# Three groups of projection tiles walk their weight rows in another order and at other places

## The chip, the cores and the metric

The kernel runs on one core of one Trainium2 chip. The metric is the device time of one execution in microseconds (us). The program's inputs and outputs lie in the chip's main memory (HBM); weights come in by DMA while the matrix engine (TensorE, "PE" in the profile) works on those that came before.

## The reference

One inference step of a hybrid decoder layer over 336 token columns: 16 meta tokens, 256 prompt tokens and 8 x 8 sample tokens. Cut to what matters here:

```python
h = rms_norm(x, norm_w)
proj = h @ w_in        # z | x,B,C | dt | B | C | h | SiLU gate | gate a | gate b
xbc = silu(causal_dwconv(xbc, conv_prev, ssd_conv_w) + ssd_conv_b)
y = ssd_chunked(xs, dt, log_a, bm, cm, state, chunk) + d_skip * xs
y_a = gated_group_rms_norm(y, z, ssd_norm_w) @ w_ssd_out
y_b = (sc_b * causal_dwconv(sc_c * sc_h) * silu(sc_z)) @ w_sconv_out
merged = sigmoid(g_a) * y_a + sigmoid(g_b) * y_b
out = rms_norm(x + merged @ w_o, final_norm_w)
```

The model width is 2048, so every projection sums over 16 blocks of 128 rows. All of it is float32.

## The kernel before

**Precision and tiles.** Each operand is split into a high and a low part that TensorE multiplies at its quicker float32 setting ("fp32r"): high by high, high by low, low by high. One output tile of 128 columns (`unit`, L136) takes the weights in two halves of 8 row blocks. For each half, `wblk` (L97) fetches 512 KB into `wraw` by a DMA on the SP queue, ScalarE (ACT) copies it to `whi`, and VectorE (DVE) writes the remainder to `wlo`. Then `mm` (L131) issues 24 matmuls: 3 passes over 8 row blocks. So one tile is 48 matmuls of 128x128 weights by 320, 324 or 336 token columns, all into one PSUM tile `pj`.

**Places in memory.** The row blocks of `whi` and `wlo` are `WS` = 144 floats (576 bytes) apart, and `spaced` (L94) puts the whole tile at a shift of 16 floats (64 bytes) times `at`. The token blocks of `hx` are 336 floats (1344 bytes) apart; tiles of 336 columns begin at a block's start, those of 324 columns 48 bytes further, and the projections of 320 columns 64 bytes further. The constants `AT_V`, `AT_Y`, `AT_O`, `AT_X`, `AT_U` = 1, 3, 3, 1, 2 (L91) are shifts.

**The walk.** `terms` (L117) lists the 24 matmuls of a half. A whole number as `plan` walks the eight row blocks upwards by one, starting at that number. A tuple walks by its step: `SEVEN` (L115) starts at block 6, goes down by two, and turns (a step of 7 or 5) so that odd and even blocks take turns in fours.

**Stages.** In order: an opening stage (L238) while the input arrives; 48 short-convolution tiles; the "gates" of branch b (L453 to L461), 16 gate tiles of 320 columns, each followed by a tile of `w_sconv_out` (`wsc`); the SSD stage, which weaves `z_units`, `conv_units`, `out_units` and the scan's own small matmuls over eight groups; then branch a's gates; and the last stage (L859 to L868), 14 tiles of `w_o` over the merged activations, with a short tail for the last 256 columns. In the SSD stage `conv_tile` (L477) projects the 32 "x tiles" (j below 32, four for each group) with 336 columns, the B tiles (j from 32) with 336, and the C tiles with 324.

**What orders the work.** Each engine runs its own list in order and waits on semaphores. The list is made by a scheduler in the tile layer that places instructions by its own estimates of when their inputs are ready. At the last stage's start L830 (ACT) and L831 (DVE) write the merged activations into `hx`, block 0 to block 15, and the matmuls of the first `w_o` tile read them.

Of the kernel before, what the change touches and what calls it, by code (L numbers as in the profile page):

```python
# [16 lines left out]
META = 16  # L17
TC = 12
TV = T - META
# [30 lines left out]
def tile_hybrid_step(ctx, tc, xT, w0, w1, w2, wdt, wso, wsc, wo, cmask, vec, hvec, convst, sconvst, xe_, fwe, h0T,  # L50
# [23 lines left out]
    hhi, hlo = hx[:, 0], hx[:, 1]  # L74
# [12 lines left out]
    def col(base, i):  # L87
        return V[:, base + i:base + i + 1]

    latest = {}  # L90
    AT_V, AT_Y, AT_O, AT_X, AT_U = 1, 3, 3, 1, 2  # L91
# [4 lines left out]
    def wblk(src, at=0):  # L96
        raw = wp.tile([P, 1024], F32, name="wraw")  # L97
        nc.sync.dma_start(raw, src)
        raw = raw.rearrange("p (k m) -> p k m", m=P)
        hi, lo = (spaced(name, at) for name in ("whi", "wlo"))  # L100
        latest["act"] = nc.scalar.activation(hi, raw, AF.Copy).ins  # L101
        latest["dve"] = nc.vector.tensor_tensor(lo, raw, fb(hi), sub).ins  # L102
        return hi, lo
# [11 lines left out]
    SEVEN, FIVE, ON = (6, (7, 5, 5, 5), -2), (6, (5, 5, 5, 5), -2), (None, (5, 5, 5, 5), -2)  # L115

    def terms(plan, half, hi, lo, xh, xl, nk):  # L117
        if not isinstance(plan, tuple):
            return [(w, x, (k + plan) % nk) for w, x in ((hi, xh), (hi, xl), (lo, xh)) for k in range(nk)]
        first, turns, step = plan  # L120
        k, out = first if half == 0 and first is not None else row[0] + step, []
        for i, (w, x) in enumerate(((hi, xh), (hi, xl), (hi, xl), (hi, xh), (lo, xh), (lo, xh))):
            if i in (2, 5):
                k += turns[2 * half + i // 5] - step
            for _ in range(4):
                out.append((w, x, k % nk))
                k += step
        row[0] = out[-1][2]
        return out

    def mm(out, hi, lo, xh, xl, base, nk, k0, first, last, plan=0, half=0):  # L131
        for i, (w, x, k) in enumerate(terms(plan, half, hi, lo, xh, xl, nk)):
            latest["pe"] = nc.tensor.matmul(out, w[:, base + k], x(k0 + k), start=first and i == 0,  # L133
                                            stop=last and i == 3 * nk - 1).ins

    def unit(src, xh, xl, n, plan=0, at=0):  # L136
        pt = ps.tile([P, 512], F32, name="pj")
        for half in range(2):
            hi, lo = wblk(src[:, half * 1024:half * 1024 + 1024], at)
            mm(pt[:, :n], hi, lo, xh, xl, 0, 8, half * 8, half == 0, half == 1, plan, half)  # L140
        return pt[:, :n]

    def proj(src, t0, plan=0, at=0):
        return unit(src, lambda k: hhi[:, k, t0:T], lambda k: hlo[:, k, t0:T], T - t0, plan, at)
# [44 lines left out]
    with tc.tile_pool(name="pa", bufs=2) as pa:  # L189
# [33 lines left out]
        for k in range(KT):  # L223
            split = nc.scalar.activation(uhi[:, k, :], ya[:, k, :], AF.Copy, scale=yan[:, k:k + 1])
            rest = nc.vector.scalar_tensor_tensor(ulo[:, k, :], ya[:, k, :], yan[:, k:k + 1], fb(uhi[:, k, :]), mult, sub)
            if k % 2 == 0:
                hi = wp.tile([P, WB], F32R, name="whi")
                lo = wp.tile([P, WB], F32R, name="wlo")
# [222 lines left out]

        tab = tables(pa)
        for m in range(KT):  # L453
            pg = proj(w2[80 + m], META)
            th = pa.tile([P, TV], F32, name="thg", tag="thz")
            nc.scalar.activation(th, pg, AF.Tanh, scale=0.5)
            py = unit(wsc[m], lambda k: vhi[:, k, :], lambda k: vlo[:, k, :], TV, 7, AT_V)
            nc.vector.scalar_tensor_tensor(th, th, 1.0, py, add, mult)
            nc.sync.dma_start(mb_d[m], th)
            next(tab, None)  # L460
# [6 lines left out]
    with tc.tile_pool(name="pb", bufs=2) as pb:  # L467
# [9 lines left out]
        def conv_tile(src, j, t0, out, cs):  # L477
            if t0:
                pp = proj(src, t0, SEVEN)
            else:  # L480
                pp = proj(src, t0, FIVE if j < 32 and j % 4 == 3 else SEVEN, AT_X)
            pad = pads[npad[0] % 2]
            npad[0] += 1
            smp = pad[:, 275:363].rearrange("p (b t) -> p b t", t=11)
            nc.scalar.activation(pad[:, 3 + t0:275], pp[:, :272 - t0], AF.Copy)  # L485
            nc.scalar.activation(smp[:, :, 3:11], pp[:, 272 - t0:].rearrange("p (b t) -> p b t", t=8), AF.Copy)
            nc.gpsimd.tensor_copy(smp[:, :, 0:3], cs[:, 1:9, :])  # L487
            nc.gpsimd.tensor_copy(cs[:, 0, :], pad[:, 272:275])  # L488
            nc.gpsimd.tensor_copy(cs[:, 1:9, :], smp[:, :, 8:11])
            i0 = META if t0 else 0  # L490
            acc = pb.tile([P, 360], F32, name="cacc")
            nc.scalar.activation(acc[:, i0:], pad[:, i0:360], AF.Identity, bias=col(V_CB, j), scale=col(V_CW, 4 * j))
            for k in range(1, 4):
                nc.vector.scalar_tensor_tensor(acc[:, i0:], pad[:, i0 + k:360 + k], col(V_CW, 4 * j + k),  # L494
                                               acc[:, i0:], mult, add)
            th = pb.tile([P, 360], F32, name="cth", bufs=1)
            nc.scalar.activation(th[:, i0:], acc[:, i0:], AF.Tanh)  # L497
            nc.vector.scalar_tensor_tensor(out[:, i0:272], th[:, i0:272], 1.0, acc[:, i0:272], add, mult)
            nc.vector.scalar_tensor_tensor(
                out[:, 272:].rearrange("p (b t) -> p b t", t=8),  # L500
                th[:, 272:360].rearrange("p (b t) -> p b t", t=11)[:, :, 3:11], 1.0,
                acc[:, 272:360].rearrange("p (b t) -> p b t", t=11)[:, :, 3:11], add, mult)

        def conv_units(g, st):
            cs = pb.tile([P, 6, 9, 3], F32, name="cs")
            nc.sync.dma_start(cs, convst[:, g])
            BT = st["BT"] = pb.tile([P, T], F32, name="BT")
            conv_tile(w1[64 + g], 32 + g, 0, BT, cs[:, 4])
            yield
            CT = st["CT"] = pb.tile([P, T], F32, name="CT")  # L510
            conv_tile(w1[72 + g], 40 + g, 12, CT, cs[:, 5])
            yield
            xs = st["xs"] = pb.tile([P, 4, T], F32, name="xs", tag=f"xs{g % 2}", bufs=1)
            for t in range(4):
                conv_tile(w1[32 + 4 * g + t], 4 * g + t, 0, xs[:, t, :], cs[:, t])
                yield
            nc.sync.dma_start(convo[:, g], cs)
# [19 lines left out]
        def ssd(g, st):  # L537
# [67 lines left out]
            def state(c, terms):  # L605
                pst = ps.tile([P, 512], F32, name="ms") if c == 2 else ps.tile([P, 4, 512], F32, name="yb", bufs=1)[:, 0]
                for i, (lhs, rhs) in enumerate(terms):
                    nc.tensor.matmul(pst, lhs, rhs, start=i == 0, stop=i == len(terms) - 1)  # L608
                if c:
                    nc.vector.tensor_tensor(hst[c], hst[c], pst, add)  # L610
                else:
                    nc.scalar.activation(hst[c], pst, AF.Copy)
# [215 lines left out]
    with tc.tile_pool(name="pc", bufs=3) as pc_:  # L828
# [30 lines left out]
        for m in range(KE):  # L859
            xr = pc_.tile([P, TV], F32, name="xr")  # L860
            nc.sync.dma_start(xr, xk[:, m, META:])
            po = unit(wo[m], lambda k: hhi[:, k, :TV], lambda k: hlo[:, k, :TV], TV, at=AT_O)
            nc.vector.scalar_tensor_tensor(ya[:, m, :TV], po, 0.5, xr, mult, add)
            s_ = pc_.tile([P, TV], F32, name="sqf") if m else sacc
            nc.scalar.activation(s_, ya[:, m, :TV], AF.Square)
            if m:
                nc.gpsimd.tensor_tensor(sacc, sacc, s_, add)  # L867
            nc.scalar.activation(ya[:, m, :TV], ya[:, m, :TV], AF.Copy, scale=col(V_FW, m))  # L868
        nc.sync.dma_start(xe[:, :PT], xe_)
        nc.sync.dma_start(fw[:, :PT], fwe.partition_broadcast(P))  # L870
        for m in range(KE, KT):
            xr = pc_.tile([P, TV], F32, name="xr")[:, :NA]
            nc.sync.dma_start(xr, xk[:, m, META:META + NA])
            po = ps.tile([P, 512], F32, name="pj")
            for half in range(2):
# [6 lines left out]
                for wide in ((True, False), (False, True))[half]:  # L882
                    for k in range(8):
                        w, x = (h, hx[:, :, 8 * half + k, :NA]) if wide else (l, hhi[:, 8 * half + k, :NA])
# [141 lines left out]
def _build(shapes):  # L1026
    import concourse.bacc as _bacc
    import concourse.tile as _tile

    nc = _bacc.Bacc("TRN2", target_bir_lowering=False, num_devices=1, dynamic_dma_scratch_size=8192)  # L1030
    args = [nc.dram_tensor(n, s, F32, kind="ExternalInput").ap() for n, s in shapes]
    args += [nc.dram_tensor(n, s, F32, kind="ExternalOutput").ap() for n, s in _OUTS]
    with _tile.TileContext(nc) as tc:
        tile_hybrid_step(tc, *args)
    return nc
# [23 lines left out]
```

## Time and profile before

| | |
|---|---|
| median of 2 runs | 1780.62 us (1780.04 to 1781.2) |
| the profiled execution | 1779.76 us |
| its span, first to last instruction | 1777.9 us |
| PE busy / weight loads busy | 1768.5 us / 1751.2 us |
| DVE, ACT, POOL busy | 1145.9, 828.6, 392.9 us |
| matmuls | 13006, of which 11280 by L133 |

One profiled execution was read as a page and through views of its trace: stretches of time with the busy time of each engine, instructions in order of time (neighbours of one kind merged, with start, length and count), and groups by line. A 320-column matmul is shown 0.30 us long, but the next one starts well before it ends, so the pace of matmuls is read from starts: in a merged row of n matmuls it is (length minus the last one's 0.30 or 0.32 us) divided by n - 1.

### The profile page before, as it was taken

How to read it: one execution, taken by the hardware profiler on the slowest of the kernel's cores; microseconds unless marked ns; L12 is line 12 of the kernel's file. 1: busy time of each engine (PE TensorE's matmuls, PEld its weight loads, DVE VectorE, ACT ScalarE, POOL GpSimd, SP SyncE). 2: the span in 40 equal slices, each digit the busy share in tenths (PEclk: the TensorE clock that was granted, in tenths of full speed). 3: DMA queues.
4: the chain of work that ended last, by engine and by line, in shares of the span. 5: the costliest groups of instructions: out<-in, count | busy, mean ns of one | idle time of the engine just before them, and what ended most of it. 6: DMA issues, size and time to landing. Idle time of an engine off the chain costs nothing.

```text
span 1777.9 us, 32410 instructions
## 1 busy us (share of the span) xinstructions
PE 1768.5 (99%) x13006; PEld 1751.2 (98%) x13006; DVE 1145.9 (64%) x1696; ACT 828.6 (47%) x1269; POOL 392.9 (22%) x398
## 2 busy tenths in 40 slices
PE   9999999999999999999999999999999999999998
PEld 9999999999999999999999999999999999999998
DVE  7845544544643335668587787877878778776644
ACT  6433333333333334645656454564546556343543
POOL 0100000000000001253253433434334252400012
PEclk9999999999999999999999999999999999999999
DMA  7444444444444557467466574665756657577553
GB/s 258 152 155 153 156 153 155 151 155 155 157 162 159 169 166 237 151 187 248 160 211 222 184 247 155 213 218 183 249 158 215 211 176 254 156 247 220 190 182 128
DMA packets 117286, 331.33 MB, mean 186 GB/s; under 512 B 20944, under 2 KB 37904, under 8 KB 117136
## 3 DMA queue, kind: packets, MB, share of 16 engines
q1 hardware_dynamic: 116272, 327.89, 56.9%
q8 instruction: 102, 1.67, 0.4%
q10 hardware_dynamic: 864, 1.38, 0.2%
q14 instruction: 48, 0.39, 0.1%
HBM read 296.34 MB, written 32.88 MB: 185 GB/s over the span
## 4 chain that ended last, share of the span: by engine, by line
PE 88%; DVE 5%; DMA 4%; ACT 2%; issue 1%; POOLq 0%; SPq 0%; POOL 0%; ACTq 0%; DVEq 0%
PE pj L133 81%; DMA wraw<-w 3%; PE yb L673 2%; DVE wlo L102 1%; DMA ssms<-h 1%; DVE h L739 1%; PE ms L659 1%; PE pj L238 1%; ACT whi L101 1%; DVE cacc L494 1%; ACT W L582 1%; PE yb L608 1%; PE pj L885 1%; PE ms L238 0%; PE yb L911 0%
## 5 line engine op out<-in xcount | busy, mean ns | idle before, releaser
L133 PE MATMUL pj<-hx,whi 128*128 128x320 f32 (+2 forms) x5760 | 894.7, 308 | 0.0
L133 PEld LDWEIGHTS pj<-hx,whi 128*128 128x128 f32 x5760 | 846.9, 188 | 4.7 <-ACT pad L485 1.7
L102 DVE TENSOR_TENSOR wlo<-wraw,whi 128x1024 fp32r<-128x1024 f32 x470 | 597.6, 1272 | 384.6 <-ACT whi L101 200.7
L101 ACT ACTIVATE whi<-wraw 128x1024 fp32r<-128x1024 f32 x470 | 496.5, 1057 | 719.3 <-PE pj L133 589.4
L133 PE MATMUL pj<-hx,wlo 128*128 128x320 f32 (+2 forms) x2880 | 473.5, 307 | 0.0
L133 PEld LDWEIGHTS pj<-hx,wlo 128*128 128x128 f32 x2880 | 430.7, 188 | 0.0
L619 POOL TENSOR_TENSOR h<-h,decS 128x512 f32<-128x512 f32 x64 | 76.4, 1227 | 141.8 <-PE ms L659 141.8
L133 PE MATMUL pj<-yh,whi 128*128 128x320 f32 x512 | 95.3, 308 | 2.6 <-DVE yan L767 1.4
L261 POOL COPY SCS<-up 128x2 f32<-128x2 f32 x16 | 20.9, 1303 | 346.1 <-DVE up L255 315.9
L133 PE MATMUL pj<-yl,whi 128*128 128x320 f32 x512 | 93.6, 305 | 0.0
L133 PE MATMUL pj<-yh,wlo 128*128 128x320 f32 x512 | 93.4, 304 | 0.0
L494 DVE SCALAR_TENSOR_TENSOR cacc<-pad,V,cacc 128x360 f32<-128x360 f32 (+1 forms) x144 | 89.7, 623 | 2.0
L767 DVE TENSOR_TENSOR yan<-yan,pj 128x320 f32<-128x320 f32 x112 | 53.8, 484 | 55.8 <-PE pj L133 55.5
L133 PEld LDWEIGHTS pj<-yh,whi 128*128 128x128 f32 x512 | 78.9, 188 | 5.9 <-DVE yan L767 2.2
L487 POOL COPY pad<-cs 128x24 f32<-128x24 f32 x48 | 56.2, 1172 | 126.4 <-DVE cacc L494 117.7
L133 PEld LDWEIGHTS pj<-yl,whi 128*128 128x128 f32 x512 | 78.7, 188 | 0.0
L133 PEld LDWEIGHTS pj<-yh,wlo 128*128 128x128 f32 x512 | 78.5, 188 | 0.0
L488 POOL COPY cs<-pad 128x3 f32<-128x3 f32 x48 | 45.4, 946 | 79.0 <-ACT pad L485 78.5
L867 POOL TENSOR_TENSOR sacc<-sacc,sqf 128x320 f32<-128x320 f32 x13 | 15.6, 1198 | 187.4 <-DMA wraw<-wo 120.5
L591 POOL TENSOR_TENSOR xe<-xdt,tet 128x512 f32<-128x512 f32 (+1 forms) x24 | 30.4, 1266 | 100.3 <-DVE xdt L562 100.3
L497 ACT ACTIVATE cth<-cacc 128x360 f32<-128x360 f32 (+1 forms) x48 | 24.0, 499 | 43.2 <-DVE cacc L494 42.9
L133 PE MATMUL pj<-vhi,wlo 128*128 128x320 f32 x256 | 41.5, 304 | 0.0
(284 smaller groups left out, 1634.6 us busy)
## 6 DMA issues: line engine op xcount, KB each, us to landing
wraw<-w SPq DMA_DIRECT2D x346, 512.0 KB, 3.8
wraw<-wso SPq DMA_DIRECT2D x64, 512.0 KB, 3.6
wraw<-wsc SPq DMA_DIRECT2D x32, 512.0 KB, 3.8
h<-h0T SPq DMA_DIRECT2D x32, 512.0 KB, 5.0
ssms<-h SPq DMA_DIRECT2D x32, 512.0 KB, 4.1
wraw<-wo SPq DMA_DIRECT2D x32, 512.0 KB, 3.9
xq_d<-xe SPq DMA_DIRECT2D x16, 320.0 KB, 3.3
W<-ac_d SPq DMA_DIRECT2D x8, 576.0 KB, 6.5
```

Source lines behind the costliest of these rows:

```text
L101: latest["act"] = nc.scalar.activation(hi, raw, AF.Copy).ins
L102: latest["dve"] = nc.vector.tensor_tensor(lo, raw, fb(hi), sub).ins
L133: latest["pe"] = nc.tensor.matmul(out, w[:, base + k], x(k0 + k), start=first and i == 0, stop=last and i == 3 * nk - 1).ins
L261: nc.gpsimd.tensor_copy(SCS[:, j, 0, :], up[:, 256:258])
L487: nc.gpsimd.tensor_copy(smp[:, :, 0:3], cs[:, 1:9, :])
L488: nc.gpsimd.tensor_copy(cs[:, 0, :], pad[:, 272:275])
L494: nc.vector.scalar_tensor_tensor(acc[:, i0:], pad[:, i0 + k:360 + k], col(V_CW, 4 * j + k), acc[:, i0:], mult, add)
L497: nc.scalar.activation(th[:, i0:], acc[:, i0:], AF.Tanh)
L591: nc.gpsimd.tensor_tensor(split(xe[c][:n]), split(xdt[c][:n]), bc(hv(tet[:n, c, :], g), [n, 8, HP]), mult)
L619: nc.gpsimd.tensor_tensor(split(h0[b]), split(h0[b]), bc(hv(decS[:, b, :], g), [P, 8, HP]), mult)
L673: nc.tensor.matmul(yb[q * HP:(q + 1) * HP, t, t0:t0 + n], x[:, h * HP:(h + 1) * HP], w[:, h, :], start=i == 0, stop=i == 3)
L767: nc.vector.tensor_tensor(ya[:, m, :TV], ya[:, m, :TV], pp[:, :TV], add)
```

## The change

Three groups of tiles get another walk and another shift. Branch b's gates walk by `SEVEN` instead of upwards by one, at shift m % 4 instead of 0. The x tiles walk by one, upwards for even groups and downwards for odd ones, instead of by `SEVEN` or `FIVE`, at a shift that goes through 2, 3, 0, 1 (upwards) or 0, 1, 2, 3 (downwards) instead of 1. The `w_o` tiles walk downwards by one (0, 7, 6, ... 1) instead of upwards, at shift m % 4 instead of 3. `terms` learns to read a negative whole number as a downward walk. The number of instructions, their sizes and the sums are the same.

```diff
     def terms(plan, half, hi, lo, xh, xl, nk):
         if not isinstance(plan, tuple):
-            return [(w, x, (k + plan) % nk) for w, x in ((hi, xh), (hi, xl), (lo, xh)) for k in range(nk)]
+            return [(w, x, ((k if plan >= 0 else -k) + plan) % nk) for w, x in ((hi, xh), (hi, xl), (lo, xh)) for k in range(nk)]
...
         for m in range(KT):
-            pg = proj(w2[80 + m], META)
+            pg = proj(w2[80 + m], META, SEVEN, m % 4)
...
             if t0:
                 pp = proj(src, t0, SEVEN)
             else:
-                pp = proj(src, t0, FIVE if j < 32 and j % 4 == 3 else SEVEN, AT_X)
+                if j < 32:
+                    up = j // 4 % 2 == 0
+                    pp = proj(src, t0, 0 if up else -8, (j + (2 if up else 0)) % 4)
+                else:
+                    pp = proj(src, t0, SEVEN, AT_X)
...
         for m in range(KE):
...
-            po = unit(wo[m], lambda k: hhi[:, k, :TV], lambda k: hlo[:, k, :TV], TV, at=AT_O)
+            po = unit(wo[m], lambda k: hhi[:, k, :TV], lambda k: hlo[:, k, :TV], TV, -8, m % 4)
```

In the lists of ACT, DVE, POOL and SP nothing moves, and in PE's list only one place does: the start of the last stage. Elsewhere the same matmuls stand in the same groups, and only the addresses inside the groups differ. Here is PE's list before at the first `w_o` tile (`pj_18102`, its weights `whi_18105` and `wlo_18106`, then `whi_18135` and `wlo_18136`) and the start of the second (`pj_18168`); a row's "waits" names the engine whose work it waits for, Activation being ACT:

```order
L133 MATMUL pj_18102<-hx_80,whi_18105 128x320 [waits Activation_49] x8
L133 MATMUL pj_18102<-hx_80,whi_18105 128x320 [waits DVE_49] x8
L133 MATMUL pj_18102<-hx_80,wlo_18106 128x320 x8
L133 MATMUL pj_18102<-hx_80,whi_18135 128x320 [waits Activation_49] x8
L133 MATMUL pj_18102<-hx_80,whi_18135 128x320 [waits DVE_49] x8
L133 MATMUL pj_18102<-hx_80,wlo_18136 128x320 x8
L133 MATMUL pj_18168<-hx_80,whi_18171 128x320 x16
```

Each matmul of the first two passes of a half waits for its own block of `hx`, in the order in which ACT and DVE write the blocks. PE's list of the changed kernel at the same place:

```order
L133 MATMUL pj_18102<-hx_80,whi_18105 128x320 [waits Activation_49] x2
L133 MATMUL pj_18102<-hx_80,whi_18105 128x320 x6
L133 MATMUL pj_18102<-hx_80,whi_18105 128x320 [waits DVE_49] x2
L133 MATMUL pj_18102<-hx_80,whi_18105 128x320 x6
L133 MATMUL pj_18102<-hx_80,wlo_18106 128x320 x8
L133 MATMUL pj_18102<-hx_80,whi_18135 128x320 [waits Activation_49] x2
L133 MATMUL pj_18102<-hx_80,whi_18135 128x320 x6
L133 MATMUL pj_18102<-hx_80,whi_18135 128x320 [waits DVE_49]
L133 MATMUL pj_18168<-hx_80,whi_18171 128x320 x2
L133 MATMUL pj_18102<-hx_80,whi_18135 128x320 [waits DVE_49]
L133 MATMUL pj_18102<-hx_80,whi_18135 128x320 x6
L133 MATMUL pj_18102<-hx_80,wlo_18136 128x320 x8
```

Now the second matmul of a pass already waits for the half's last block (7, then 15), the six behind it need no wait of their own, and the scheduler has put two matmuls of the second tile ahead of the wait for the low part of block 15.

## Prediction

> **What bounds the kernel now.** I read the page first, engines and then the chain of waits that ended last:
>
> ```profile
> PE 1768.5 (99%) x13006; PEld 1751.2 (98%) x13006; DVE 1145.9 (64%) x1696; ACT 828.6 (47%) x1269; POOL 392.9 (22%) x398
> PEclk9999999999999999999999999999999999999999
> PE 88%; DVE 5%; DMA 4%; ACT 2%; issue 1%; POOLq 0%; SPq 0%; POOL 0%; ACTq 0%; DVEq 0%
> ```
>
> PE is busy 99% of the 1777.9 us span, at full granted clock, and it is 88% of the chain. So the time is set by the pace of matmuls, and an edit that moves only addresses can act through that pace or through a wait of PE. Next I read stretches of time (columns: start to end, length, PE busy and its matmuls, weight loads, granted clock, DMA share, GB/s) for the three groups that change: 17 tiles of the gate stage, two neighbouring tiles of 336 columns, 12 tiles of the last stage. The two of 336 columns are the x tiles' kind, from group 0.
>
> ```profile
> 551.70:667.30 115.60, 115.60 (x819) 115.60 (x818) 1.00 0.51 167
> 695.48:709.92 14.44, 14.44 (x98) 14.44 (x97) 1.00 0.66 233
> 1664.73:1746.33 81.60, 81.60 (x579) 81.60 (x578) 1.00 0.60 189
> ```
>
> I set the edges at the first matmul of a tile; the counts are two or three over the tiles' own 48 each, as matmuls overlap an edge. 115.60 / 816 and 81.60 / 576 are both 141.7 ns, and 14.44 / 96 is 150.4 ns. Scaling 141.7 ns by 336/320 gives 148.8 ns. So the gates and the `w_o` tiles run at the quickest pace that any long stretch here has, and the x tiles 1.6 ns from its scaled value. What this change could win at the most is 32 tiles x 48 x 1.6 ns = 2.5 us, 0.14% of the time. What it can lose is not bounded in that way.
>
> **What an offset is.** Each weight load runs while the matmul before it still streams its tokens. I call a tile's offset the place of the weights being loaded less the place of the tokens being streamed, in units of 64 bytes, modulo 4, from the built program's addresses. Weight blocks are 9 units apart and token blocks 21, so a step of one block changes the difference by 12 and leaves the offset alone: it is constant through a walk, but at `SEVEN`'s turns. Before, every 320-column tile that repeats has offset 1 (gates, `wsc`, z, `w_ssd_out`, `w_o`), the x tiles have 0, the 324-column tiles 3. After it, gates have 2, 3, 0, 1 in turn, `w_o` tiles 0, 1, 2, 3, x tiles 0, 1, 2, 3. So 12 of 16 gates, 10 of 14 `w_o` tiles and 24 of 32 x tiles get an offset that no long run of their shape shows. The price has to come from places where offsets vary:
>
> ```profile
> 19.32 0.31 PE L238 MATMUL ms<-uhi,whi 128*128 128x320 f32 x1
> ...
> 26.82 0.31 PE L238 MATMUL pj<-uhi,whi 128*128 128x324 f32 x1
> 461.14 0.32 PE L357 MATMUL pj<-hx,wd 128*128 128x336 f32 x1
> ...
> 465.93 0.31 PE L358 MATMUL pj<-hx,wd 128*128 128x336 f32 x1
> 1169.56 1.30 PE L133 MATMUL pj<-hx,wlo 128*128 128x320 f32 x8
> ...
> 1177.23 1.32 PE L133 MATMUL pj<-hx,wlo 128*128 128x320 f32 x8
> ```
>
> In the opening stage the offset jumps from matmul to matmul: 51 steps in 7.50 us, 147.1 ns each, at 320 and 324 columns alike. At the dt projection (336 columns, jumping too) 31 steps take 4.79 us, 154.5 ns each. The last two rows are one pass of eight in two z tiles of one group, same offset, same walk: (1.30 - 0.30) / 7 = 143 ns and (1.32 - 0.30) / 7 = 146 ns, at the print's two decimals. So pace is not a matter of column count alone.
>
> **The change part by part.**
>
> *Gates and `w_o`, new offsets.* Bounds for a 320-column matmul: 0 (an offset held constant costs nothing) and 147.1 - 141.7 = 5.4 ns. Nothing suggests a gain, since 141.7 ns is the quickest pace shown. I take 4.0 ns, nearer the upper row: the opening stage is the only place that shows 320 columns at offsets other than 1 many times over. Gates: 12 x 48 x 4.0 ns = 2.3 us (0 to 3.1). `w_o`: 10 x 48 x 4.0 ns = 1.9 us (0 to 2.6).
>
> The Trainium skill, "TensorE: Matmul & The Clock Gate", Part 2, step-by-step, says: "Loading the next tile's weights doesn't steal SBUF read bandwidth from the running matmul." By that rule this whole term is nothing, and the sum below would be 4.2 us lower. The 147.1 ns of the opening stage do not sit well with it, but there the offset jumps and here it stays.
>
> *x tiles.* Bounds per matmul, against 150.4 ns: 148.8 - 150.4 = -1.6 ns and 154.5 - 150.4 = +4.1 ns. I take +1.0 ns for the 24 tiles with a new offset, near the middle: 24 x 48 x 1.0 ns = 1.2 us (-1.8 to +4.7). The eight that keep offset 0 lose `SEVEN`'s turns; taken at nothing (-0.6 to +1.6).
>
> *Entries.* A tile that follows one of another offset or walk starts slower:
>
> ```profile
> 118.15 2.07 PE L133 MATMUL pj<-hx,whi 128*128 128x324 f32 x13
> 125.09 2.17 PE L133 MATMUL pj<-hx,whi 128*128 128x324 f32 x14
> ```
>
> Both are `SEVEN` tiles of 324 columns, the first behind a 320-column tile at another offset, the second behind one of its own kind: (2.07 - 0.30) / 12 = 147.5 ns against (2.17 - 0.30) / 13 = 143.8 ns, so about 0.04 us an entry. Gates and `wsc` tiles alternate, so 31 entries there turn from equal to unequal, and 13 among the `w_o` tiles; x tiles already enter unequal at most places. 44 x 0.04 us is 1.8 us as the upper end, 0 the lower; I take 1.0 us.
>
> *The first `w_o` tile.* Walking downwards, the second matmul of each pass needs the half's last block:
>
> ```profile
> 1656.72 2.50 DVE L831 TENSOR_TENSOR hx<-yan,hx 128x320 fp32r<-128x320 f32 x6
> 1657.92 1.72 PE L133 MATMUL pj<-hx,whi 128*128 128x320 f32 x11
> ...
> 1660.28 1.05 ACT L101 ACTIVATE whi<-wraw 128x1024 fp32r<-128x1024 f32 x1
> 1660.34 2.90 DVE L831 TENSOR_TENSOR hx<-yan,hx 128x320 fp32r<-128x320 f32 x7
> 1661.23 0.45 ACT L830 ACTIVATE hx<-yan 128x320 fp32r<-128x320 f32 x1
> 1661.33 2.43 PE L133 MATMUL pj<-hx,whi 128*128 128x320 f32 x16
> 1663.17 1.22 DVE L102 TENSOR_TENSOR wlo<-wraw,whi 128x1024 fp32r<-128x1024 f32 x1
> 1167.20 1.96 PE L133 MATMUL pj<-hx,whi 128*128 128x320 f32 x12
> ```
>
> The tile starts at 1657.92 us, its second half at 1661.33 us. Upwards, the low part of block 15 is read by that half's 16th matmul, at 1661.33 + 15 x 0.142 = 1663.46 us, and DVE ends it at 1663.24 us: just in time. Downwards it is read by the 10th, at 1662.61 us, 0.63 us early. Two matmuls of the next tile now stand ahead of that wait (0.28 us), which leaves 0.35 us. On the way, block 7's low part (ended 1659.22 us, wanted 1657.92 + 9 x 0.142 = 1659.20 us) and block 15's high part (ended 1661.68 us, wanted 1661.47 us) stop PE for parts of that same time. A stop costs its restart besides: the last row is a tile's first 12 matmuls behind a break, (1.96 - 0.30) - 11 x 0.142 = 0.10 us slow. I take 0.5 us, from 0.3 to 0.9. Queued behind each waiting matmul is all of PE's list; nobody else waits for that long, as ACT and DVE have written the second tile's weights by then.
>
> *ACT, DVE, DMA.* Their lists do not move, only the place that `whi` and `wlo` are written to. At 1.05 and 1.22 us a half tile against PE's 24 x 0.142 = 3.4 us they hide behind PE. I cost them at nothing; twice as long, they would still hide here.
>
> *Sum.* 2.3 + 1.9 + 1.2 + 1.0 + 0.5 = 6.9 us. The profiled execution took 1779.76 us (span 1777.9 us and 1.9 us around it), 0.86 us below the median of the runs, 1780.62 us. So 1786.7 us by that execution, 1787.5 us by the median; I write 1787.
>
> **The rivals.**
>
> *A constant offset is free (the skill's rule above).* Only jumps cost, as in the opening stage. For it: three long runs at offsets 1, 0 and 3 (320, 336 and 324 columns) lie within about 1% of one pace per column. Against: the x tiles' 1.6 ns, the only offset 0. Then stop 0.5 us and entries 0 to 1.8 us stand, and x tiles bring 0 to -2.5 us: -2.0 to +2.3 us, 1778.6 to 1782.9 us, about 1781. Chance 0.25.
>
> *Every new offset costs what the jumping rows cost.* 22 x 48 x 5.4 ns + 32 x 48 x 4.1 ns = 5.7 + 6.3 us, with entries 1.8 and stop 0.9 us: 14.7 us, 1795 us. For it: those rows; against: each tile would have to stay in the state in which others spend their first dozen matmuls. Chance 0.15.
>
> *Slower by over 2%: at a new offset the weight load is no longer hidden.* The place is the 46 tiles with new offsets, 2208 matmuls. The restart above, 0.10 us, is what a load that starts late costs once; at each of them it makes 221 us, 2002 us in all. It decides from 36 us on, 16 ns a matmul; the highest row, the dt projection's, is 154.5 - 148.8 = 5.7 ns over its scaled pace. Chance 0.02.
>
> The forecast itself has 0.58.
>
> **How the numbers follow.** The likeliest case is 1787 us; its own bounds are 1781 (all lower ends but the stop's) to 1794 us. For the range I take 1781 to 1794 us: it leaves out some half of the first rival (0.13) and the upper rivals' better part. A change of 2% is about what a measurement of this kernel tells from none, and 36 us either way is beyond all but the last rival: faster 0.01 (at most 2.5 us is to be won), same 0.97, slower 0.02.
>
> **What would show it.** In the changed kernel's stretches: gate and `w_o` tiles at shifts with offset 1 (gate 3, 7, 11, 15; `w_o` 1, 5, 9, 13) at 6.80 us, the others near 6.99 us; x tiles between 7.14 and 7.4 us, varying with j % 4; a stop of PE in the first `w_o` tile, with DVE's L831 as its releaser. If all gates take 6.80 us, the offset term is wrong; if the stretch of the `w_o` tiles is longer with no slower tile, the stop was undersized; if other stages change pace, the addresses act where I did not look.

## The result, and the profile after

The changed kernel takes 1789.76 us (median of 2 runs, 1788.88 to 1790.63) against 1780.62 us: a ratio of 1.0056, 95% interval 1.0039 to 1.0072, 9.1 us longer. It is slower, but within 2%. The forecast was 1787 us with a range of 1781 to 1794 us.

The profiled execution took 1788.88 us, its span is 1787.1 us. The page's engines, the granted clock and the chain by engine:

```profile
PE 1778.8 (100%) x13006; PEld 1761.6 (99%) x13006; DVE 1147.0 (64%) x1696; ACT 829.6 (46%) x1269; POOL 390.5 (22%) x398
PEclk9999999999999999999999999999999999999999
PE 94%; DVE 2%; ACT 2%; DMA 1%; issue 1%; POOLq 0%; POOL 0%; ACTq 0%; DVEq 0%; SPq 0%
```

The same instructions, the same clock, the other engines as busy as before, and PE 10.3 us busier: matmuls take longer at full clock. Stretches of one tile each show where (columns: start to end, length, PE busy and matmuls, granted clock, DMA share, GB/s; the counts are two to four over 48, as neighbours overlap an edge). In this order: four gates at offsets 2, 3, 0, 1; four x tiles of an upward group (offsets 0, 1, 2, 3), four of a downward group, and four `w_o` tiles (0, 1, 2, 3).

```profile
567.21:574.27 7.06, 7.06 (x50) 1.00 0.55 176
581.08:588.12 7.04, 7.04 (x51) 1.00 0.58 186
594.95:602.01 7.06, 7.06 (x50) 1.00 0.57 182
608.82:615.89 7.07, 7.07 (x51) 1.00 0.55 172
908.61:916.05 7.44, 7.44 (x50) 1.00 0.81 233
916.35:923.52 7.17, 7.17 (x51) 1.00 0.31 110
924.27:931.75 7.48, 7.48 (x52) 1.00 0.81 285
931.75:939.28 7.53, 7.53 (x50) 1.00 0.76 234
1017.77:1025.05 7.28, 7.28 (x51) 1.00 0.73 237
1025.34:1032.62 7.28, 7.28 (x50) 1.00 0.30 108
1033.38:1040.77 7.39, 7.39 (x52) 1.00 0.83 289
1040.77:1048.24 7.47, 7.47 (x51) 1.00 0.78 229
1691.43:1698.69 7.26, 7.26 (x50) 1.00 0.55 182
1698.69:1705.67 6.98, 6.98 (x50) 1.00 0.56 158
1705.67:1712.79 7.12, 7.12 (x51) 1.00 0.59 181
1712.79:1719.75 6.96, 6.96 (x51) 1.00 0.57 166
```

Gates and `w_o` tiles took 6.80 us before. Now all four gates take 7.04 to 7.07 us, the one at offset 1 too. Downward `w_o` tiles take 7.26 us at offset 0, 7.09 or 7.12 at 2, and 6.96 to 6.98 at 1 and 3. The x tiles differ by offset and by direction. The restarts behind the scan's small matmuls are in these lengths, so I also give the mean distance from one matmul's start to the next's behind a tile's first twelve matmuls (so in all that follows): before it was 149.9 ns for all 32; now upward it is 155.0, 148.3, 153.7, 155.0 ns at offsets 0 to 3, downward 151.7, 151.7, 151.7 (once 153.4), 153.6 ns.

Added up over all tiles of both traces, from the start of each matmul to the start of the next:

| | change, us |
|---|---|
| 16 gates of branch b | +4.06 |
| the `wsc` tiles between them | +0.29 |
| x tiles | +3.60 |
| `w_o` tiles, the first one's stops included | +4.07 |
| z tiles and gates of branch a | -0.59 |
| `w_ssd_out` tiles, with the waits behind them | -1.27 |
| the rest | -1.0 |
| sum, as the spans differ | +9.1 |

So 12.0 us were lost in the tiles that the change touches and those between, and 2.9 us came back elsewhere in this execution.

### The profile page after: what moved, and what is told of

The parts are those of the page before. It is cut to its first block, busy times and chain, and to the rows that moved or that the text cites. A ratio compares the mean times of both kernels' runs of the same rounds, so it can differ in the third digit from the quotient of the medians.

```text
span 1787.1 us, 32410 instructions
## 1 busy us (share of the span) xinstructions
PE 1778.8 (100%) x13006; PEld 1761.6 (99%) x13006; DVE 1147.0 (64%) x1696; ACT 829.6 (46%) x1269; POOL 390.5 (22%) x398
## 4 chain that ended last, share of the span: by engine, by line
PE 94%; DVE 2%; ACT 2%; DMA 1%; issue 1%; POOLq 0%; POOL 0%; ACTq 0%; DVEq 0%; SPq 0%
PE pj L133 87%; PE yb L677 2%; DMA wraw<-w 1%; PE ms L663 1%; PE pj L238 1%; PE yb L612 1%; ACT whi L101 1%; DVE wlo L102 1%; ACT W L586 1%; PE pj L889 1%; PE ms L238 0%; PE ms L561 0%; PE yb L740 0%; PE yb L915 0%; DVE cacc L498 0%
## 5 line engine op out<-in xcount | busy, mean ns | idle before, releaser
L133 PE MATMUL pj<-hx,whi 128*128 128x320 f32 (+2 forms) x5760 | 901.9, 309 | 0.0
L133 PEld LDWEIGHTS pj<-hx,whi 128*128 128x128 f32 x5760 | 853.0, 188 | 4.9 <-ACT pad L489 1.7
L133 PE MATMUL pj<-hx,wlo 128*128 128x320 f32 (+2 forms) x2880 | 477.4, 308 | 0.0
L133 PEld LDWEIGHTS pj<-hx,wlo 128*128 128x128 f32 x2880 | 434.2, 188 | 0.0
L133 PE MATMUL pj<-yh,whi 128*128 128x320 f32 x512 | 95.1, 307 | 1.3 <-ACT zs L530 0.8
L133 PE MATMUL pj<-yl,whi 128*128 128x320 f32 x512 | 93.5, 304 | 0.0
L133 PE MATMUL pj<-yh,wlo 128*128 128x320 f32 x512 | 93.4, 304 | 0.0
L133 PEld LDWEIGHTS pj<-yh,whi 128*128 128x128 f32 x512 | 78.9, 188 | 4.1 <-ACT zs L530 1.3
L133 PEld LDWEIGHTS pj<-yl,whi 128*128 128x128 f32 x512 | 78.6, 188 | 0.0
L133 PEld LDWEIGHTS pj<-yh,wlo 128*128 128x128 f32 x512 | 78.5, 188 | 0.0
L133 PE MATMUL pj<-vhi,whi 128*128 128x320 f32 x256 | 41.7, 305 | 0.0
```

## The experiments

Every run is compared with runs of the kernel before on the same chip.

**The parts one by one.** `e1_gates` has only the gates' line of the change, `e2_xtiles` only the x tiles', `e3_wo` only the `w_o` tiles' (each with the new `terms` where it needs it).

```diff
# e1_gates
-            pg = proj(w2[80 + m], META)
+            pg = proj(w2[80 + m], META, SEVEN, m % 4)
# e2_xtiles
-                pp = proj(src, t0, FIVE if j < 32 and j % 4 == 3 else SEVEN, AT_X)
+                if j < 32:
+                    up = j // 4 % 2 == 0
+                    pp = proj(src, t0, 0 if up else -8, (j + (2 if up else 0)) % 4)
+                else:
+                    pp = proj(src, t0, SEVEN, AT_X)
# e3_wo
-            po = unit(wo[m], lambda k: hhi[:, k, :TV], lambda k: hlo[:, k, :TV], TV, at=AT_O)
+            po = unit(wo[m], lambda k: hhi[:, k, :TV], lambda k: hlo[:, k, :TV], TV, -8, m % 4)
```

> Only branch b's gates as in the changed kernel, the rest as before. If every group's cost is its own (theory 1), the gate tiles take 7.03 to 7.07 us as in the changed kernel, all four shifts alike, and the whole is longer by 16 x 0.25 + 8 x 0.03 = 4.3 us. If PE's later waits give time back wherever a slowdown lies (theory 2), by clearly less, 2 to 3 us.

> Only the x tiles as in the changed kernel. Theory 1 (a group's cost is its own and stays): 3.6 us longer, the sum over the 32 tiles. Theory 2 (the SSD stage gives back what its tiles lose, because PE's waits for DVE and ACT there and the slower passes of z tiles shrink): the tiles lose 3.6 us and the whole is longer by only 0.7 to 1.5 us.

> Only the w_o tiles as in the changed kernel. Theory 1: 3.9 to 4.2 us longer, tiles at 7.26 us (shift 0), 6.97 (1), 7.09 to 7.12 (2), 6.96 (3), and 0.1 to 0.2 us of it in the first tile's waits. If the first tile's stop is as large as I had it, its share is 0.5 us and the whole 4.4 us.

Measured: gates alone 1.0023 (1.0013 to 1.0034), +4.1 us; x tiles alone 1.0012 (1.0002 to 1.0022), +2.1 us; `w_o` alone 1.0020 (1.0011 to 1.0029), +3.6 us. (Each is the ratio less 1, times the median before.) Together +9.8 us, against +10.0 us for the whole change by the same reckoning, +9.1 us by its medians. The tiles' own sums are as in the changed kernel: gates +4.06 us, x tiles +3.60, `w_o` tiles +4.00. So each group's price is its own, and tile for tile the same from program to program. What of the x tiles' price reaches the whole time is not settled by this run: its interval, 0.4 to 3.9 us, holds both expected values.

**The shift without the walk.** `e4_shifts` keeps the walks of before and turns only the shifts.

```diff
-            pg = proj(w2[80 + m], META)
+            pg = proj(w2[80 + m], META, 0, m % 4)
...
-                pp = proj(src, t0, FIVE if j < 32 and j % 4 == 3 else SEVEN, AT_X)
+                pp = proj(src, t0, FIVE if j < 32 and j % 4 == 3 else SEVEN, j % 4 if j < 32 else AT_X)
...
-            po = unit(wo[m], lambda k: hhi[:, k, :TV], lambda k: hlo[:, k, :TV], TV, at=AT_O)
+            po = unit(wo[m], lambda k: hhi[:, k, :TV], lambda k: hlo[:, k, :TV], TV, at=m % 4)
```

> The four shifts in turn in all three groups, but the walks as before. If the offset is what costs (the prediction's term), 320-column tiles at offsets 0, 2 and 3 slow down by 3 to 6 ns a matmul (12 gates and 10 w_o tiles, near 6.95 to 7.1 us each, those at offset 1 at 6.80 us) and the whole gets 3.5 to 6 us longer. If the walk is what costs and the shift does nothing, all 320-column tiles stay at 6.80 us and the whole within 1 us of before. x tiles at SEVEN with four shifts: 7.2 us if only the walk counts; 7.1 to 7.45 us by shift if the offset counts.

Measured: 1.0045 (1.0030 to 1.0060), +8.0 us, more than I expected, because of the x tiles: under `SEVEN` (at offset 2 `FIVE`) they stand at 149.9, 152.6, 155.9 and 153.9 ns at offsets 0 to 3 and lose 4.4 us. Four neighbouring upward gates at offsets 1, 2, 3, 0, one tile each:

```profile
566.18:573.14 6.96, 6.96 (x50) 1.00 0.55 173
580.10:587.01 6.91, 6.91 (x50) 1.00 0.53 177
593.84:600.64 6.80, 6.80 (x51) 1.00 0.55 182
607.44:614.48 7.04, 7.04 (x51) 1.00 0.52 170
```

The offset does cost, with walk, direction and instructions as before: 7.04 us at 0, 6.91 us at 2. Offsets 1 and 3 each come at two paces: 141.7 ns as in the third row (6.80 us), or 144.9 ns at offset 1 (the first row) and 146.6 at offset 3 (the `w_o` tiles). So both are true: the offset counts, and, with the gates' 7.07 us at offset 1 under `SEVEN`, the walk counts too. It is not `SEVEN`'s turns, where the offset jumps, that carry this cost: in the gate at 608.82 us of the changed kernel the first seven distances, ahead of its first turn, already average 146.9 ns.

**Difference or place.** `e6_moved` puts 64 empty bytes ahead of `hx`, so that `hx` and everything allocated behind it, weights included, move by one unit.

```diff
-    hx = keep.tile([P, 2, KT, T], F32R, name="hx")
+    hx = keep.tile([P, 2 * KT * T + 16], F32R, name="hx")[:, 16:].rearrange("p (i k t) -> p i k t", i=2, t=T)
```

> The kernel before with hx and all that lies behind it, weights included, 64 bytes further on: every difference between weights and tokens stays, every address moves. If the difference counts, no tile changes its pace and the time is within 0.5 us of before. If places by themselves count, gates or w_o tiles leave 6.80 us by 0.15 us or more each and the whole gets 2 us or more longer.

Measured: 1.0003 (0.9993 to 1.0013). The `w_o` tiles stay at 6.80 us, the repeating gates too, the x tiles at 149.9 ns. Here are the first 13 `w_o` tiles in one stretch, 88.40 / 624 = 141.7 ns a matmul:

```profile
1656.24:1744.64 88.40, 88.40 (x626) 1.00 0.58 187
```

So, for a move by one unit, what counts is the difference of the two places, not the places.

**Whose direction.** In `e7_opposite` the `w_o` weights lie in reversed block order and 11 units apart, in another pool, so that weights and tokens walk in opposite directions at a constant offset. The products and sums are the same. (The helpers' new parameters and the new block order of `w_o` in main memory are not shown.)

```diff
-            po = unit(wo[m], lambda k: hhi[:, k, :TV], lambda k: hlo[:, k, :TV], TV, at=AT_O)
+            po = unit(wo[m], lambda k: hhi[:, k, :TV], lambda k: hlo[:, k, :TV], TV, 0 if m < 6 else -8, m % 4, 176, pc_)
...
-            latest["pe"] = nc.tensor.matmul(out, w[:, base + k], x(k0 + k), start=first and i == 0,
+            latest["pe"] = nc.tensor.matmul(out, w[:, nk - 1 - k if back else base + k], x(k0 + k), start=first and i == 0,
```

> w_o tiles whose weights lie in reversed order and 11 units apart, so that weights and tokens walk in opposite directions and the offset still stays constant: the first six tiles with tokens upwards, the last eight with tokens downwards, at offsets 2, 3, 0, 1 in turn. If only the offset between load and stream and the tokens' direction count, upward tokens give 141.7 ns at offset 1 and more elsewhere, downward tokens the changed kernel's numbers: 151.7 ns at 0, 145.0 at 1, 147.8 at 2, 145.0 at 3. If the direction of the weights matters by itself, the two lists do not repeat; if it is the weights' direction alone, the first six tiles show the downward numbers and the last eight the upward ones. Because the weights lie in another pool, the first of these tiles starts later; the whole time is not compared.

One execution, 1791.51 us; its first `w_o` tile starts late, so the whole time is not compared. In order of time, some passes of this kernel's `w_o` tiles (start, length, engine, line, names, count). The distance from one shown row to the next is one tile, but two from the third to the fourth. The first two rows start tiles with upward tokens at offsets 1 and 2 (the third ends the second of them), the last five rows start tiles with downward tokens at offsets 3, 0, 1, 2, 3. L134 is this kernel's number for L133:

```profile
1687.52 2.45 PE L134 MATMUL pj<-hx,xwhi 128*128 128x320 f32 x16
...
1694.34 2.48 PE L134 MATMUL pj<-hx,xwhi 128*128 128x320 f32 x16
...
1701.27 2.51 PE L134 MATMUL pj<-hx,xwhi 128*128 128x320 f32 x16
...
1715.39 2.49 PE L134 MATMUL pj<-hx,xwhi 128*128 128x320 f32 x16
...
1722.36 2.57 PE L134 MATMUL pj<-hx,xwhi 128*128 128x320 f32 x16
...
1729.62 2.49 PE L134 MATMUL pj<-hx,xwhi 128*128 128x320 f32 x16
...
1736.59 2.54 PE L134 MATMUL pj<-hx,xwhi 128*128 128x320 f32 x16
...
1743.71 2.48 PE L134 MATMUL pj<-hx,xwhi 128*128 128x320 f32 x16
```

Upward: 6.82 us at offset 1, 6.93 us at 2, as `e4_shifts` has them. Downward: 6.97 at offset 3, 7.26 at 0, 6.97 at 1, 7.12 at 2, which is the changed kernel's list. Weights that walk the other way, in other steps and in another place, change nothing. That does not make it the tokens alone: where the offset is constant, the weights' step equals the tokens' step modulo 4 units (before, 9 and 21 units up, both 1; here 11 down and 21 up, again both 1), so no run here parts the two.

**Direction or step.** `e8_threes` walks the `w_o` tiles by three blocks, the first seven upwards, the last seven downwards. Three token blocks up are 63 units, which modulo 4 is the same as 21 down.

```diff
+        if len(plan) == 1:
+            return [(w, x, k * plan[0] % nk) for w, x in ((hi, xh), (hi, xl), (lo, xh)) for k in range(nk)]
         first, turns, step = plan
...
-            po = unit(wo[m], lambda k: hhi[:, k, :TV], lambda k: hlo[:, k, :TV], TV, at=AT_O)
+            po = unit(wo[m], lambda k: hhi[:, k, :TV], lambda k: hlo[:, k, :TV], TV, (3,) if m < 7 else (-3,), m % 4)
```

> w_o tiles that walk by three blocks: the first seven upwards (tokens 63 units a step) at offsets 0, 1, 2, 3, 0, 1, 2, the last seven downwards (or 105 up, at the wrap) at offsets 1, 2, 3, 0, 1, 2, 3. If what counts of the walk is the tokens' step modulo 4 units, three blocks up (63 is 3 modulo 4, as 21 down is) repeat the list of the downward walk by one: 151.7, 145.0, 147.8, 145.0 ns at offsets 0 to 3; three blocks down repeat that of the upward walk by one: 146.5 to 146.9 at 0, 141.7 or 144.9 at 1, 143.9 at 2, 146.6 (or 141.7) at 3. If it is the direction, the two lists change places. If it is the jump in memory itself, all fourteen stand near 147 ns, as the walk by two does.

One execution, 1784.08 us. Four of its tiles, three up at offsets 0 and 1, then three down at offsets 0 and 1:

```profile
1659.06:1666.32 7.26, 7.26 (x50) 1.00 0.48 153
1666.32:1673.30 6.98, 6.98 (x51) 1.00 0.76 256
1729.49:1736.54 7.05, 7.05 (x51) 1.00 0.55 189
1736.54:1743.50 6.96, 6.96 (x51) 1.00 0.54 168
```

Mean distance of starts: three up 151.7, 145.0, 148.3, 145.0, 151.7, 145.0, 147.8 ns at offsets 0, 1, 2, 3, 0, 1, 2; three down 141.6, 144.0, 146.6, 146.8, 145.0, 143.9, 146.6 ns at offsets 1, 2, 3, 0, 1, 2, 3. Three up is the list of one down, three down that of one up, to the tenth of a nanosecond. It is the step modulo 4 units, not its direction or length. Every token step here is a whole number of 21-unit blocks, so 12, 28 or 84 units would sort the steps alike; 4 is the smallest modulus that does.

| 320 columns, ns: tokens' step modulo 4 | offset 0 | 1 | 2 | 3 |
|---|---|---|---|---|
| 1 (one up, three down) | 146.3 to 146.9 | 141.7 or 144.9 | 143.9 | 146.6 or 141.7 |
| 2 (`SEVEN`) | 147.1 | 147.7 | 147.1 to 147.9 | 146.3 to 147.0 |
| 3 (one down, three up) | 151.7 | 145.0 | 147.8 to 148.3 | 145.0 |

Taking the offset from the weights of the matmul itself, not from those being loaded, would only shift each row of this table; the runs do not choose between the two.

**Two paces at one offset.** `e9_const3` sets all `w_o` tiles to shift 1, offset 3 upwards.

```diff
-            po = unit(wo[m], lambda k: hhi[:, k, :TV], lambda k: hlo[:, k, :TV], TV, at=AT_O)
+            po = unit(wo[m], lambda k: hhi[:, k, :TV], lambda k: hlo[:, k, :TV], TV, at=1)
```

> The kernel before with all w_o tiles at shift 1, which upwards is offset 3. If offset 3 has a price of its own, all fourteen take 7.04 us (146.6 ns a matmul) and the whole is 3.3 us longer. If offsets 1 and 3 each have a quick and a slow state and a tile stays in that of the tile ahead of it, all fourteen take 6.80 us, since the gate ahead runs at 141.7 ns.

One execution, 1783.37 us. Two of its tiles, the fourth and the tenth:

```profile
1679.27:1686.31 7.04, 7.04 (x51) 1.00 0.54 167
1721.51:1728.55 7.04, 7.04 (x51) 1.00 0.59 180
```

All fourteen take 7.04 us, 3.35 us more in all, although the gate ahead runs at 141.7 ns. My guess that a tile stays in the pace of the tile ahead of it has fallen. That one offset has two lasting paces is seen (offset 3 at 6.80 us in `e4_shifts`, at 7.04 us here); what chooses between them stays open. The tile just ahead alone does not: in `e4_shifts` two `wsc` tiles, unchanged and both behind a gate at offset 0, take 6.97 us (from 559.22 us) and 6.80 us (from 614.48 us).

**A quicker walk for the 336-column tiles.** `e5_up` is the kernel before with its 32 x tiles and 8 B tiles upward by one at offset 1.

```diff
-                pp = proj(src, t0, FIVE if j < 32 and j % 4 == 3 else SEVEN, AT_X)
+                pp = proj(src, t0, 0, 3)
```

> The kernel before, but its 336-column tiles (32 x tiles and 8 B tiles) walk upwards by one at shift 3, which is offset 1. If walk and offset together set the pace, as the changed kernel's four fastest kinds of x tiles show (148.3 ns a matmul upwards at offset 1), each of 40 tiles goes from 7.21 or more to 7.13 to 7.17 us: 1.5 to 3 us shorter, ratio 0.9985 to 0.999. If the SSD stage gives back only in one direction (PE then waits longer for DVE and ACT), the gain is under 0.7 us.

Measured: 0.9988 (0.9978 to 0.9999), 2.1 us shorter. Two x tiles of group 0, which took 7.22 us each before:

```profile
695.38:702.50 7.12, 7.12 (x51) 1.00 0.81 309
702.50:709.62 7.12, 7.12 (x51) 1.00 0.50 163
```

The 40 tiles win 2.7 us. It is the one version here that is quicker than the kernel before, by little.

**What the SSD stage gives back.** `e10_xtiles_again` and `e11_up_again` are `e2_xtiles` and `e5_up` once more.

> The x tiles alone once more, with more rounds, to see what becomes of the tiles' 3.6 us. If the SSD stage's waits give nothing back on the whole, the tiles' 3.6 us less the 0.6 us of quicker z tiles remain: 3.0 us, ratio 1.0017. If the waits give back what one profile showed (2.4 us), 0.6 us, ratio 1.0003.

> Upward 336-column tiles at offset 1 once more, with more rounds. The tiles win 2.7 us and the z tiles 0.8 us. If the waits of PE in the SSD stage do not care, 3.5 us shorter, ratio 0.998; if PE, being quicker, waits longer there as one profile showed (2.7 us more), 0.7 us shorter, ratio 0.9996.

Measured: 1.0015 (1.0006 to 1.0023), +2.6 us, and 0.9988 (0.9979 to 0.9997), -2.1 us. For the slower x tiles "nothing given back" (3.0 us) holds and 0.6 us is excluded; for the quicker ones neither 3.5 nor 0.7 us is. The weight loads of the `w_ssd_out` tiles, by groups (busy time, mean of one | idle time before them, and what ended it), of before, of `e2_xtiles` and of `e11_up_again`:

```profile
L133 PEld LDWEIGHTS pj<-yh,whi 128*128 128x128 f32 x512 | 78.9, 188 | 5.9 <-DVE yan L767 2.2 <-ACT zs L526 1.9 <-ACT whi L101 0.2
```

```profile
L133 PEld LDWEIGHTS pj<-yh,whi 128*128 128x128 f32 x512 | 79.0, 188 | 4.1 <-ACT zs L530 1.8 <-DVE yan L771 0.8 <-issue 0.2
```

```profile
L133 PEld LDWEIGHTS pj<-yh,whi 128*128 128x128 f32 x512 | 78.9, 188 | 8.4 <-ACT zs L526 5.0 <-DVE yan L767 1.9 <-issue 0.2
```

These waits are the place. They stand at 5.9, 6.4, 6.0, 4.6, 6.5, 6.8 and 5.7 us in seven profiles with the old x tiles (before, `e3_wo`, `e1_gates`, `e6_moved`, `e7_opposite`, `e8_threes`, `e9_const3`), at 4.1, 4.1, 4.9 and 4.7 us with slower ones (the changed kernel, `e2_xtiles`, `e10_xtiles_again`, `e4_shifts`) and at 7.1 and 8.4 us with quicker ones (`e5_up`, `e11_up_again`). The direction fits a part given back, some 1 to 2 us. But 4.6 to 6.8 us with old tiles shows that single executions wander as far, and the timed runs cannot tell the part from none. That stays open.

## Why the prediction was right, and where it was not

**What bounds the kernel** held: the loss lies in the pace of matmuls at full clock, and ACT, DVE and DMA hid as before.

**Gates, new offsets** (2.3 us, 0 to 3.1): measured 4.06 us, over the upper end. The failing step is "12 x 48": I counted four gates at offset 1 as free. Under `SEVEN` none is: all sixteen stand near 147 ns, 5.3 ns over the old pace, which is inside my bound of 5.4 ns for one matmul. The walk had a price that I did not look for, since I took it that a constant offset is all that a walk leaves to the pace.

**`w_o`** (1.9 us, 0 to 2.6): measured 4.07 us with the stops. Again offsets 1 and 3 cost 3.3 ns each where I had offset 1 free, and offset 0 costs 10 ns, twice the upper bound. A row in which offsets jump was no upper end: a constant offset can be worse than a mixture.

**x tiles** (1.2 us for those with new offsets and 0 for the eight others): measured 3.60 us for all. The bounds of single matmuls (148.8 and 154.5 ns) were nearly right, 148.3 and 155.0 ns. The value near the middle was not: of eight kinds one is quicker than before and seven are slower.

**Entries** (1.0 us): the `wsc` tiles show theirs plainly, 0.03 us in eight of the sixteen, under 0.01 us in the other eight, 0.29 us in all. Those of the gates and `w_o` tiles are inside the sums above and were not separated, so the term as a whole is not measured.

**The first `w_o` tile** (0.5 us, 0.3 to 0.9): it came where forecast, near the lower end of its size. Its row in the changed kernel:

```profile
1665.40 2.90 DVE L835 TENSOR_TENSOR hx<-yan,hx 128x320 fp32r<-128x320 f32 x7
...
1666.61 2.60 PE L133 MATMUL pj<-hx,whi 128*128 128x320 f32 x15
```

DVE ends block 15's low part at 1668.30 us and the matmul that reads it starts at 1668.37 us, with the two matmuls of the next tile ahead of it. The three stops and restarts make about 0.33 us (distances of 252, 185, 251 and 233 ns where 147 to 150 are usual). In the length of the tile only 0.16 us of that remains over another tile at offset 0 (7.42 against 7.26 us), because behind the stops it ran at 145 to 150 ns instead of 151.7. The profile's list of PE's waits names no releaser there, so that DVE's L835 (L831 before) ended the last stop is read from these times.

**What I had no term for**: 2.9 us less outside those tiles in this execution. Of it, 0.59 us are z tiles that leave their slower pace; it is the same in the profiles of `e2_xtiles` and `e10_xtiles_again`. So the mechanism, the pace at new offsets, was right, and that the sum came near, 6.9 against 9.1 us, is partly luck: gates, `w_o` with its stops and x tiles were sized too small (by 1.8, 1.7 and 2.4 us), and the 2.9 us, some of which may be the wandering of single executions, hid about half of that. The tiles alone, 12.0 us, would still have been inside the range.

**The range.** Its lower bound does not follow from the terms: all lower ends but the stop's add up to -1.8 - 0.6 + 0.5 = -1.9 us, which is 1779 us and not 1781. The upper ends add up to 14.7 us, 1794 to 1795 us, as stated. The result lies inside either way. Nor is 2% what these runs can tell: the interval here, 1.0039 to 1.0072, tells 0.6% from none.

**The rivals.** "A constant offset is free" falls by `e4_shifts`: with the same walk, the shift alone takes a tile from 6.80 to 7.04 us. The Trainium skill's page "TensorE: Matmul & The Clock Gate" (Part 2, step-by-step) states that a weight load does not steal the running matmul's read bandwidth. These 7.04 us do not agree with it as a rule for the time, though no run here shows what the load and the stream contend for. "Every new offset costs what the jumping rows cost" was near in its total for the tiles, 12.0 us, for another reason. The weight load that is no longer hidden did not come: apart from the first `w_o` tile's stops no tile lost more than 10 ns a matmul. What I said would show the forecast wrong in a part, equal gates, did show: they are equal, but at 7.05, not at 6.80 us.

## What to carry to other kernels

Where PE is busy throughout, read its pace from matmul to matmul, per tile, and compare it with the best pace that the same shape has anywhere in the trace: addresses alone moved it here by up to 7% (151.7 against 141.7 ns). When a walk or a layout changes, two numbers have to be kept, the place of the weights being loaded less that of the tokens being streamed, and the step of the walk, both modulo 256 bytes here; fixing one and turning the other is a change of pace. Rows in which a quantity varies from one instruction to the next bound what a mixture costs, not what a constant bad value costs.

## What the runs showed that I had not expected

- At one offset the step of the walk counts too, modulo 4 units of 64 bytes: three blocks up give exactly the paces of one block down. The weights' direction, spacing and pool did not count in `e7_opposite`; their step modulo 4 goes with the tokens'.
- A pace belongs to a tile almost to the nanosecond: apart from tiles that wait and a few z tiles (up to 0.16 us), the same tile in different programs has the same length, while whole executions of one program differ by several us (1776.33 to 1782.59 us for the kernel before on one chip).
- One offset can hold two lasting paces: 141.7 or 144.9 ns at offset 1, 141.7 or 146.6 ns at offset 3, both with tokens upwards.
- The quickest pace of 336 columns, 148.3 ns, is just below the 148.8 ns that I scaled from 320 columns.
